# Hybrid mixer of a two-layer decoder: every second conv tile of the values and of the state space in another PSUM pool, with a new table of priority shifts

## The chip, the cores and the metric

The kernel runs on one core of one Trainium2 chip. The metric is the device time of one execution in microseconds, as the median of several runs. The profile is of one execution, taken by the hardware profiler.

## The reference

Two layers, 256 tokens of width 1024, in float32. Each layer is a feed-forward block, a mixer, and a second feed-forward block, each followed by a layer norm. Layer 0 has the hybrid mixer, which this case is about; layer 1 has a sparse attention.

```python
proj = x @ w_in                               # 256 x 1024 by 1024 x 5664
gdn_qkv, gdn_z, gdn_b, gdn_a, ssd_z, ssd_xbc, ssd_dt = split(proj)
# branch A: gated delta rule
qkv = silu(causal_conv(gdn_qkv, gdn_conv_w))  # 4 taps along the tokens, per channel
q, k, v = split(qkv)                          # 512, 512 and 1024 channels
o_a = rms_normalize(gated_delta_rule(q, k, v, g, beta)) * norm_w * silu(gdn_z)
# branch B: state-space scan
xbc = silu(causal_conv(ssd_xbc, ssd_conv_w) + ssd_conv_b)
xs, bm, cm = split(xbc)                       # 1024, 256 and 256 channels
o_b = rms_normalize((ssd_scan(xs, dt, a, bm, cm) + xs * d_skip) * silu(ssd_z)) * norm_w
return concat(o_a, o_b) @ w_out
```

## The kernel before

The whole computation is first written down as a list of operations (class Plan). Each operation belongs to an engine and has a priority, which is its place in the list plus a shift from the table SHIFTS: for each of the six stages (0 and 2 the feed-forward blocks of layer 0, 1 the hybrid mixer, 3 and 5 the feed-forward blocks of layer 1, 4 the attention) and each engine, a run-length list of (count, shift) over that engine's operations. A planner (Plan.order) then walks a cost model and, among the operations that are ready, gives each engine the one that can start first, and among equals the one with the lowest priority number. The result is a fixed order for each engine and a fixed place for each buffer; the chip then runs it with semaphores. So a change of a buffer's pool or of a shift moves the order of everything that follows.

PSUM's eight banks are three pools: ps with two banks, mp with two, acc with four. A tile takes a bank when its first operation is to start and gives it back after its last. Tiles of ps form one queue. Tiles of mp form one queue for each strand (STRANDS), all on the same two banks.

Matrices are split into a high and a low float32r part (whi, wlo from raw; x is held in the same way), and a product is three matmuls: high by high, high by low, low by high. Weights are loaded from DRAM by SP's queue into raw, rounded by ACT into whi, and VectorE makes wlo by subtraction.

In the hybrid mixer the keys and queries are projected and convolved first. Then five strands are woven together into the list (weave): delta (the delta rule's blocks, on acc), space, gate, space2 and out_a. Strand space holds the convolutions of this case: gdn_conv for the eight tiles of the values (128 channels each, 24 matmuls of 256 columns, tile by proj_steps), and then twelve state-space tiles (bm, cm and xs, by two_steps: eight matmuls of 512 columns and eight of 256). Each tile's bank is then read out by conv_tile: for a value tile ACT copies it to src; for a state-space tile ACT copies its second half and VectorE adds the first to it. The taps follow in SBUF (tiles cv). Strand gate makes the gate zs of the state-space branch, four tiles of 24 matmuls in ps, each read out by ACT. Strand space2 is the state-space scan; its products, and some of its transposes, are on mp. It waits until the xs tiles are there, and ends in the second half of the mixer's output, oT[1], which the last output matmuls of the mixer need.

turn is a transpose that does not use TensorE: ACT separates the float32 words into halves, a DMA from SP's queue transposes them, ACT puts them together.

Of the kernel before, what the change touches and what calls it, by code (L numbers as in the profile page):

```python
# [20 lines left out]
P = 128  # L21
# [31 lines left out]
        "tensor": [(18, -578), (1, 84), (2, -1851), (5, 0), (2, 407), (32, 0), (11, -1907), (2, 262), (32, 0), (22, 201), (5, 382), (5, 1394),  # L53
# [4 lines left out]
        "vector": [(2, -16), (1, 0), (4, 451), (1, 4), (1, -1802), (4, 0), (1, -739), (8, 0), (1, -2831), (3, 0), (8, 275), (1, 0), (2, 22), (7, 0),  # L58
            (1, -640), (1, 0), (1, -31), (12, -213), (2, 0), (18, -135), (1, -485), (1, -700), (4, 0), (12, -453), (6, 94), (3, 16), (1, -381),
            (2, -590), (5, 31), (3, 13), (4, 0), (6, -82), (1, -177), (3, -235), (2, 378), (4, -178), (10, -583)],  # L60
        "scalar": [(3, 756), (1, 0), (6, -699), (1, -20), (4, -2184), (2, 0), (2, -327), (6, -381), (1, -2057), (3, -1945), (1, -153), (12, 82),
            (2, 328), (1, -276), (1, -88), (1, -1), (2, -105), (2, -5), (4, 0), (1, -13), (2, -258), (16, 0), (1, -130), (2, 415), (1, 361),
            (1, -453), (12, 0), (2, 37), (14, 389), (1, -116), (1, 230), (2, 204), (4, -315), (1, -74), (7, -49), (1, -67), (2, -235), (5, -23),
            (2, 0), (10, -693)],
        "gpsimd": [(1, 451), (1, 0), (1, -714), (4, -48)],
        "sync": [(6, 0), (3, -1981), (1, -3772), (6, 0), (1, -85), (5, 1078), (2, 496), (1, 0), (56, 1116)],
    },
    1: {
        "tensor": [(218, 0), (26, -298), (75, 0), (2, 188), (1, 0), (1, 70), (1, 99), (2, 0), (4, -88), (4, 228), (1, 350), (2, -643), (29, 0),
# [10 lines left out]
        "vector": [(78, 0), (10, 241), (1, 3), (5, 408), (9, 40), (18, 0), (1, 273), (2, 293), (29, -903), (3, 392), (3, 504), (2, -456), (1, -320),  # L80
# [5 lines left out]
        "scalar": [(38, 0), (1, -321), (1, -310), (1, -130), (61, 0), (1, 520), (1, 322), (2, 0), (4, -46), (1, -21), (6, -66), (12, -449), (1, -10),  # L86
# [4 lines left out]
        "gpsimd": [(4, 57), (2, 43), (1, 53), (2, 0), (5, -40)],  # L91
        "sync": [(4, 297), (44, 0), (1, 452), (6, 230), (2, -3), (5, -355), (16, 3), (1, -364), (4, 0), (1, 6)],
    },
    2: {
        "tensor": [(74, 0), (1, -329), (1, -126), (2, -149), (9, 0), (1, -35), (5, 0), (1, -161), (5, 95), (20, -68), (2, 0), (9, 124), (8, -1221),
# [5 lines left out]
        "vector": [(30, 0), (1, -835), (1, 0), (1, -1084), (1, -565), (1, -599), (30, 0), (1, 98), (4, 72), (4, -1), (1, 35), (4, 768), (1, -608),  # L101
            (2, -480), (1, -541), (17, 42), (9, -118), (2, 0), (1, -101), (1, -146), (1, -144), (4, 0), (6, 871), (1, -135), (1, 1018), (7, 0),
            (2, 895), (7, 0), (1, -347), (2, -2074), (1, 0), (1, -1455), (5, -1745), (2, -1637), (1, -1605), (1, -2549), (1, 15), (1, -1586)],
        "scalar": [(10, 0), (22, 33), (3, -320), (1, 0), (35, 41), (1, -17), (2, -24), (1, -257), (13, 0), (1, 133), (5, 0), (3, -6), (1, -35),
            (5, -118), (5, -5), (5, -4), (1, 1040), (3, 42), (15, 0), (1, -175), (1, -348), (1, -1923), (1, -1471)],
    },
    3: {
        "tensor": [(3, 2), (22, 110), (7, 0), (2, 258), (1, -281), (18, 0), (2, 122), (23, 0), (2, -861), (8, 48), (1, -351), (139, -36), (1, 1919),
# [66 lines left out]
V_TURN, X_TURN = (1, 1), (1, 0)  # L175
O_TURN, Y_TURN, Q_TURN = (1, 1), (0, 1), (1, 1, 1, 1)
S_TURN = (0, 0, 1, 0, 0, 0, 1, 1)
L_TURN = (0, 0, 0, 0, 0, 0, 0, 0, 0, 0)
RUN = 1
MASKED = (1, 0)  # L180

# [610 lines left out]
class K:  # L792
# [1355 lines left out]
    def nsa(self, x, then):  # L2148
# [237 lines left out]
        def attend(g, b):  # L2386
# [3 lines left out]
            PT = {}  # L2390
# [235 lines left out]
```

## Time and profile before

| | |
|---|---|
| Median of 3 runs | 1056.72 us (1056.31 to 1056.89) |
| The profiled execution | 1058.01 us |
| Its span, first to last instruction | 1056.3 us |
| Instructions in the span | 15912 |
| Mean granted TensorE clock | 0.999 |

Engines in the profile: PE is TensorE's matmul, PEld its weight load (which overlaps PE), DVE is VectorE, ACT ScalarE, POOL GpSimd, SP SyncE. Operations are shown as out<-in by the names of the tiles. All operations are emitted by one helper, so they have one line (L757) and are told apart by their tiles. The row of a wait names who waited, for whom, how long in total, how often, and the longest. Times in rows are microseconds from the span's start unless ns is said. A float32 matmul or transpose is recorded as two matmuls, a float32r one as one.

### The profile page before, as it was taken

The page shows a single profiled execution, that of the slowest core. Times are in us where ns is not written, and L with a number is a line of the kernel's source. Part 1 is how long each engine was busy: PE and PEld are TensorE (multiplying, and loading weights), DVE is VectorE, ACT ScalarE, POOL GpSimd, SP SyncE. Part 2 cuts the span into 40 slices and gives each one's busy share as a digit, 9 for nine tenths or more (in the row PEclk, how much of TensorE's full clock was granted, in tenths as well). Part 3 has the DMA queues.
Part 4 walks back from the last instruction along what each step waited for, and adds up shares of the span by engine and source line. Part 5 has one row for each costly group of instructions (what it writes and reads, how often), then busy time and mean ns, then how long its engine had stood idle before and what let it go on. Part 6 is the DMA issues. An engine that isn't in the chain of part 4 may idle for free.

```text
span 1056.3 us, 15912 instructions
## 1 busy us (share of the span) xinstructions
PE 1043.7 (99%) x5686; PEld 868.4 (82%) x5686; DVE 1006.7 (95%) x1430; ACT 772.0 (73%) x1155; POOL 84.9 (8%) x122
## 2 busy tenths in 40 slices
PE   9999999999999999999999999999999999999997
PEld 7888888899898888888888888788887778888886
DVE  6999999898999989999999999999988999999987
ACT  7676976379867966868876678687477976878880
POOL 1001000001000201110000200000010101000100
PEclk9999999999999999999999999999999999999999
DMA  9999986744962798999779845978664355689991
GB/s 322 296 285 269 286 287 193 222 114 114 203 198 72 227 283 235 285 283 264 275 229 316 236 160 179 261 253 278 212 202 148 110 184 136 202 232 248 297 276 40
DMA packets 185977, 235.35 MB, mean 223 GB/s; under 512 B 54365, under 2 KB 115498, under 8 KB 185898
## 3 DMA queue, kind: packets, MB, share of 16 engines
q1 hardware_dynamic: 176650, 216.51, 65.1%
q0 software_dynamic: 9248, 17.83, 9.8%
q8 instruction: 45, 0.74, 0.3%
q14 instruction: 34, 0.28, 0.1%
HBM read 221.30 MB, written 1.07 MB: 211 GB/s over the span
## 4 chain that ended last, share of the span: by engine, by line
PE 52%; DVE 14%; ACT 3%; issue 3%; DMA 3%; POOL 1%; DVEq 0%; ACTq 0%; POOLq 0%
PE ps L757 18%; PE acc L757 18%; PE mp L757 15%; DVE wlo L757 5%; DMA turned<-words 2%; DVE cv L757 2%; ACT whi L757 2%; DVE arena L757 1%; DVE raw L757 1%; DVE h L757 1%; DMA G<-rates 1%; DVE qs L757 1%; DVE sw L757 0%; POOL arena L757 0%; DVE y L757 0%
## 5 line engine op out<-in xcount | busy, mean ns | idle before, releaser
L757 DVE TENSOR_TENSOR wlo<-raw,whi 128x1024 fp32r<-128x1024 f32 (+2 forms) x447 | 522.2, 1207 | 5.5 <-ACT whi L757 4.9
L757 ACT ACTIVATE whi<-raw 128x1024 fp32r<-128x1024 f32 (+1 forms) x428 | 424.0, 1044 | 53.0 <-DVE raw L757 37.3
L757 PE MATMUL ps<-whi,x 128*128 128x512 f32 (+1 forms) x544 | 144.2, 384 | 0.2 <-DVE F L757 0.2
L757 PEld LDWEIGHTS ps<-whi,x 128*128 128x128 f32 x544 | 98.2, 188 | 18.2 <-DVE x L757 0.3
L757 DVE TENSOR_TENSOR raw<-raw,raw 128x1024 f32<-128x1024 f32 x94 | 112.1, 1218 | 0.3
L757 PE MATMUL ps<-x,whi 128*128 128x512 f32 (+2 forms) x464 | 104.6, 340 | 0.7 <-ACT cv L757 0.3
L757 PE MATMUL acc<-wlo,gh 128*128 128x512 f32 x253 | 99.1, 392 | 0.2 <-DVE wlo L757 0.2
L757 PE MATMUL acc<-whi,gl 128*128 128x512 f32 x253 | 97.9, 392 | 0.0
L757 PE MATMUL acc<-whi,gh 128*128 128x512 f32 x253 | 95.9, 392 | 0.0
L757 PEld LDWEIGHTS ps<-x,whi 128*128 128x128 f32 (+1 forms) x464 | 77.6, 187 | 10.2 <-DVE cv L757 0.6
L757 PE MATMUL acc<-whi,x 128*128 128x512 f32 x256 | 82.1, 404 | 1.0 <-DVE x L757 1.0
L757 PE MATMUL mp<-whi,x 128*128 128x512 f32 x288 | 78.3, 391 | 0.0
L757 PE MATMUL ps<-wlo,x 128*128 128x512 f32 (+1 forms) x272 | 77.7, 380 | 0.0
L757 PE MATMUL mp<-whi,fhi 128*128 128x512 f32 x192 | 75.1, 391 | 0.3 <-ACT whi L757 0.3
L757 PE MATMUL mp<-whi,flo 128*128 128x512 f32 x192 | 74.8, 390 | 0.0
L757 POOL DMA_DIRECT2D raw<-in_ffn_w_in_dram x34 | 41.1, 1216 | 337.6 <-DMA raw<-in_ffn_w_in_dram 205.1
L757 PE MATMUL ps<-x,wlo 128*128 128x256 f32 (+1 forms) x344 | 66.5, 284 | 0.0
L757 PE MATMUL acc<-whi,g 128*128 128x512 f32 x192 | 63.4, 392 | 0.0
L757 PEld LDWEIGHTS mp<-whi,x 128*128 128x128 f32 x288 | 53.2, 188 | 11.7 <-ACT su L757 0.6
L757 PE MATMUL mp<-wlo,fhi 128*128 128x512 f32 x192 | 59.4, 392 | 0.1
L757 PEld LDWEIGHTS acc<-whi,x 128*128 128x128 f32 x256 | 47.8, 190 | 11.6 <-DVE x L757 1.4
L757 PEld LDWEIGHTS ps<-wlo,x 128*128 128x128 f32 x272 | 49.5, 188 | 8.7 <-DVE wlo L757 0.2
(330 smaller groups left out, 1850.3 us busy)
## 6 DMA issues: line engine op xcount, KB each, us to landing
raw<-in_ffn_w_in_dram SPq DMA_DIRECT2D x162, 512.0 KB, 6.2
raw<-in_ffn_w_out_dram SPq DMA_DIRECT2D x88, 512.0 KB, 6.1
raw<-in_hyb_w_in_dram SPq DMA_DIRECT2D x44, 512.0 KB, 5.4
raw<-in_ffn_w_in_dram POOLq DMA_DIRECT2D x34, 512.0 KB, 9.1
raw<-in_ffn_w_in_dram SPq DMA_DIRECT2D x52, 256.0 KB, 4.7
raw<-in_hyb_w_out_dram SPq DMA_DIRECT2D x16, 512.0 KB, 4.4
raw<-in_nsa_w_in_dram SPq DMA_DIRECT2D x10, 512.0 KB, 5.4
raw<-in_nsa_cmp_w_dram SPq DMA_DIRECT2D x8, 512.0 KB, 3.9
```

Source lines behind the costliest of these rows:

```text
L757: r = getattr(getattr(nc, eng), fn)(*[res(a) for a in args], **{k: res(a) for k, a in kw.items()})
```

## The change

Ten conv tiles move from ps to mp: of each pair of value tiles and of each pair of state-space tiles the second. Which pool each takes is now a table in the source, H_BANKS: two entries for the values, two for the state space, two for the z gate (both ps, as it was). The table of shifts is replaced as a whole, in all six stages and for all engines. Two further tables, R_TURN and P_TURN, would send the attention's rotated queries and its probabilities through turn in place of TensorE's transposes; all their entries are 0. For this turn takes a list of parts as well as one tile.

```diff
 SHIFTS = {
     0: {
-        "tensor": [(18, -578), (1, 84), (2, -1851), (5, 0), (2, 407), (32, 0), (11, -1907), (2, 262), (32, 0), (22, 201), (5, 382), (5, 1394),
+        "tensor": [(15, -61), (2, -377), (2, -329), (9, 0), (45, 343), (1, 0), (2, 8), (1, 17), (39, 0), (1, 686), (1, 0), (1, 9), (1, -376),
...
+R_TURN = (0, 0, 0, 0)
+P_TURN = (0, 0, 0, 0, 0, 0, 0, 0, 0, 0, 0, 0, 0, 0, 0, 0, 0, 0, 0, 0, 0, 0, 0, 0)
+H_BANKS = ('ps', 'mp', 'ps', 'mp', 'ps', 'ps')
...
     def turn(self, out, src):
-        n = src.ids.size // P
+        n = out.ids.size // P
...
-        self.nc.scalar.activation(w, src.words(), AF.Copy)
+        parts = src if isinstance(src, list) else [src]
+        k = n // len(parts)
+        for j, part in enumerate(parts):
+            self.nc.scalar.activation(w[:, :, j * k:(j + 1) * k], part.words(), AF.Copy)
...
     def z_gate_steps(self, x, w_in, c0, zs, gated):
...
             for b in range(2):
-                ps = self.bank("ps")
+                ps = self.bank(H_BANKS[4 + b])
...
         def space():
...
-            yield from gdn_conv("v", [(8 + n, vT[n // 4][:, n % 4, :]) for n in range(8)])
+            yield from gdn_conv("v", [(8 + n, vT[n // 4][:, n % 4, :]) for n in range(8)], H_BANKS[:2])
...
                 for e in range(2):
...
-                    ps = self.bank("ps")
+                    ps = self.bank(H_BANKS[2 + e])
                     yield from self.two_steps(x, w, ps)
```

The number of entries of the shift table, by stage, is 144, 279, 131, 71, 229 and 186 before, and 134, 289, 196, 146, 238 and 137 after. In stages 2 and 3 the table before had none for POOL and SP, the one after has.

More of the change, by code (lines that the diff above doesn't have):

```diff
@@ L61 @@
[L61 to L65, printed above, removed]
@@ L94 @@
-    2: {
-        "tensor": [(74, 0), (1, -329), (1, -126), (2, -149), (9, 0), (1, -35), (5, 0), (1, -161), (5, 95), (20, -68), (2, 0), (9, 124), (8, -1221),
[5 rows of a table removed]
[L101 to L105, printed above, removed]
-    },
@@ L107 @@
-    3: {
-        "tensor": [(3, 2), (22, 110), (7, 0), (2, 258), (1, -281), (18, 0), (2, 122), (23, 0), (2, -861), (8, 48), (1, -351), (139, -36), (1, 1919),
[3 rows of a table removed]
-        "vector": [(52, 0), (34, 1991), (2, 173), (4, 0), (6, 226), (4, 252), (4, -448), (2, 0), (1, -650), (3, -6), (2, -113), (3, 0), (36, 32)],
-        "scalar": [(58, 84), (1, -212), (21, 0), (18, 277), (1, -2210), (1, -2642)],
-    },
-    4: {
-        "tensor": [(1, 883), (6, 167), (6, 0), (13, 147), (88, 0), (2, 311), (2, 0), (1, -255), (1, 0), (1, -126), (6, 0), (2, -147), (1, 67),
[9 rows of a table removed]
-        "vector": [(1, -92), (24, 166), (1, 0), (1, 389), (2, 37), (1, 0), (10, 247), (1, -35), (1, -74), (1, 0), (2, -47), (28, 0), (1, 154),
-            (11, -1223), (11, 0), (2, 389), (1, 1045), (11, 292), (2, 323), (13, 0), (4, -238), (1, 39), (1, 0), (1, 649), (1, 0), (9, -41),
-            (1, -243), (15, 0), (2, 279), (13, 0), (5, -2869), (1, -88)],
-        "scalar": [(2, -359), (1, -15), (10, 29), (1, -268), (12, 0), (16, -37), (3, -79), (1, -270), (32, 0), (4, -372), (1, -48), (1, -169),
[3 rows of a table removed]
-        "gpsimd": [(10, 0), (3, -606), (1, 215), (2, 190), (16, 223), (27, -11), (12, -78)],
-        "sync": [(2, 42), (11, 202), (1, 0), (6, 16), (1, -31)],
-    },
@@ L136 @@
-    5: {
-        "tensor": [(44, 0), (2, -603), (1, 0), (2, -547), (1, -969), (3, -845), (4, -758), (5, 0), (1, -362), (2, -155), (6, 0), (1, -303), (17, 0),
[7 rows of a table removed]
-        "vector": [(1, 59), (1, -81), (8, 43), (2, 649), (2, 0), (2, 873), (1, 568), (3, -419), (1, -217), (1, -16), (2, 231), (1, 239), (3, 367),
-            (9, 0), (1, -13), (5, 314), (6, 41), (1, 3), (1, 2), (2, -1), (12, 194), (1, 6), (1, 412), (1, 203), (1, 0), (1, 239), (4, -735), (1, 0),
-            (5, -25), (1, 0), (5, -844), (8, -524), (9, 0), (2, -141), (1, 0), (3, 4837), (8, -233), (1, 72), (1, -8), (4, -26), (14, 12), (1, -435),
-            (3, -250), (7, -1440)],
-        "scalar": [(1, 59), (5, 44), (1, 1), (1, 13), (1, 30), (1, 0), (1, 256), (1, 245), (1, 0), (3, 1277), (1, 0), (4, 77), (3, 953), (1, 0),
-            (6, -110), (1, 231), (3, 362), (1, -167), (7, 0), (1, 315), (35, 0), (1, -864), (26, 0), (1, 124), (5, -449), (21, 0), (7, -1270),
-            (3, -1446), (2, -1431), (1, -427), (7, -479)],
-        "gpsimd": [(1, 315), (5, -62), (1, 2)],
-        "sync": [(20, 0), (1, -123), (20, 0), (3, -484)],
+        "tensor": [(15, -61), (2, -377), (2, -329), (9, 0), (45, 343), (1, 0), (2, 8), (1, 17), (39, 0), (1, 686), (1, 0), (1, 9), (1, -376),
[3 rows of a table added]
@@ new lines @@
+        "vector": [(7, 14), (2, -284), (4, 0), (1, -285), (47, 0), (2, -251), (1, 2), (1, -215), (10, 74), (2, 427), (1, 177), (1, 511), (1, 134),
+            (2, -138), (3, 892), (19, 11), (1, 0), (1, -182), (1, -210), (2, -197), (1, -124), (4, 0), (2, -371), (1, 192), (14, 0), (1, 351),
+            (5, 0), (5, -224), (4, -353), (1, -340), (1, 15), (1, -48), (1, -722), (11, -727), (1, -220)],
+        "scalar": [(11, 0), (1, -284), (2, 0), (1, -350), (1, -312), (1, 0), (2, -271), (3, -278), (1, -461), (25, 0), (1, -282), (1, -367),
+            (1, -922), (2, 0), (21, -262), (1, -119), (30, 1), (3, -338), (2, 0), (1, -94), (2, -168), (2, -149), (1, -138), (1, -146), (3, -180),
+            (2, -28), (7, 0), (2, -117), (2, 0), (10, -501), (1, -154), (1, -409), (1, -152), (2, 0), (1, -220)],
@@ new lines @@
+        "gpsimd": [(1, 75), (1, 246), (13, -159)],
+        "sync": [(6, 0), (7, -231), (1, -103), (2, -105), (1, -193), (5, 508), (1, 276), (1, 543), (1, 76), (56, 603)],
+    },
+    1: {
+        "tensor": [(1, 357), (250, 0), (2, 162), (2, 0), (1, -218), (63, 0), (2, 757), (29, 129), (1, 636), (3, 169), (13, -171), (1, -237), (1, 33),
[10 rows of a table added]
+        "vector": [(85, 0), (1, 231), (1, 0), (1, -189), (1, 2), (9, -105), (55, 0), (3, -806), (14, 73), (5, -993), (18, 0), (1, -441), (1, -398),
[4 rows of a table added]
+        "scalar": [(49, 89), (4, 0), (3, 78), (1, 138), (33, 0), (9, 140), (1, 122), (1, 125), (1, 154), (1, 144), (5, 0), (1, 114), (1, 125),
[4 rows of a table added]
+        "gpsimd": [(4, -105), (1, -108), (1, -13), (1, -299), (1, -320), (2, -41), (3, 20), (3, -4), (1, 68), (2, 3), (1, -1846), (1, -1029)],
+        "sync": [(7, 86), (53, 0), (17, -126), (1, -45), (1, -41), (4, 21), (14, -24)],
+    },
@@ new lines @@
+    2: {
+        "tensor": [(2, -96), (1, 74), (20, 0), (25, -836), (3, 0), (1, 179), (24, -294), (1, -121), (43, 0), (1, -339), (1, -555), (1, -596), (2, 0),
[7 rows of a table added]
+        "vector": [(1, -11), (1, -253), (2, 33), (1, -36), (1, 0), (1, -86), (1, 4), (6, -772), (1, -2), (1, -33), (1, -45), (2, -150), (15, 0),
[3 rows of a table added]
+        "scalar": [(5, -29), (1, 47), (3, -1144), (7, -331), (1, -285), (7, 0), (1, -144), (1, 0), (1, 414), (1, 0), (1, -6), (17, 0), (1, -117),
+            (2, -156), (11, -68), (1, -77), (1, 121), (3, 220), (9, 106), (9, 1620), (1, -68), (4, -27), (1, -22), (3, 1419), (1, 31), (7, -72),
+            (1, -636), (3, -597), (1, 3), (16, 0), (1, 503), (7, -42), (3, 286), (1, 174), (1, 6), (1, -119), (1, -91), (1, -304)],
+        "gpsimd": [(9, 0), (1, -17)],
+        "sync": [(39, 0), (46, 51)],
+    },
@@ new lines @@
+    3: {
+        "tensor": [(33, 0), (1, 80), (1, 208), (1, 0), (2, -26), (6, -161), (1, -516), (1, -520), (4, 399), (9, 0), (1, -529), (7, 0), (8, 581),
[6 rows of a table added]
+        "vector": [(2, -119), (1, -132), (3, 0), (1, 27), (1, 167), (3, 0), (1, 967), (14, 0), (1, 323), (1, -377), (1, 310), (4, 289), (1, -130),
+            (2, 1083), (2, 95), (5, 0), (37, -1729), (1, -164), (4, -91), (17, 304), (3, -128), (2, -76), (1, 0), (1, 70), (66, 0), (1, 152),
+            (1, 127), (3, 0), (2, 186), (1, 194), (2, 67), (1, 49), (1, 48)],
+        "scalar": [(1, 0), (1, -74), (1, -103), (27, 106), (2, 0), (1, 92), (3, 0), (2, 56), (1, 163), (2, 50), (1, 55), (2, 0), (1, -916),
+            (1, -128), (1, -67), (50, 0), (1, -404), (3, -194), (1, -564), (1, -142), (1, -546), (1, -384), (36, 0), (1, -295), (1, -21)],
+        "gpsimd": [(1, 84)],
+        "sync": [(20, 0), (3, 76), (1, 90), (60, -180)],
+    },
@@ new lines @@
+    4: {
+        "tensor": [(58, 881), (11, 0), (1, 98), (3, 0), (1, 445), (7, 271), (1, -22), (2, 57), (2, -20), (3, -200), (10, -6), (1, 0), (1, 19),
[7 rows of a table added]
+        "vector": [(1, 911), (1, 452), (1, 40), (3, 367), (2, 371), (1, 29), (1, 43), (1, 18), (1, 142), (3, 695), (1, 1018), (1, 0), (1, 374),
[4 rows of a table added]
+        "scalar": [(1, 547), (11, 0), (1, 279), (1, 345), (3, 0), (2, 40), (6, 840), (1, 0), (1, -178), (11, -259), (1, 0), (1, 174), (1, -114),
[3 rows of a table added]
+        "gpsimd": [(11, 0), (1, 1181), (2, 0), (1, 1348), (40, 0), (1, -57), (1, -4), (1, 239), (1, -48), (1, 193), (1, 272)],
+        "sync": [(12, 0), (1, 282), (20, 0), (1, 55), (7, 0), (2, -128), (1, 13), (1, 1)],
+    },
@@ new lines @@
+    5: {
+        "tensor": [(48, 1446), (5, 684), (2, 152), (21, 1868), (26, 0), (5, 212), (1, 65), (4, 552), (31, 0), (4, 215), (3, 195), (1, 156), (95, 0),
[4 rows of a table added]
+        "vector": [(11, 570), (1, 573), (1, 20), (1, 0), (1, 497), (1, 452), (1, -20), (4, -323), (1, 5), (2, -60), (1, -171), (39, 133), (6, 35),
[3 rows of a table added]
+        "scalar": [(6, 0), (1, 2), (1, 10), (1, 103), (1, 0), (1, 774), (6, 0), (1, 2), (1, -523), (7, -372), (4, -325), (63, 0), (1, -170),
+            (1, -202), (1, -367), (1, 338), (7, 0), (1, -136), (1, 100), (1, 142), (5, -231), (1, 22), (1, 28), (14, 0), (1, -497), (2, -487),
+            (1, -217), (1, -211)],
+        "sync": [(44, 0), (1, -525), (45, -31)],
@@ L2243, in queries @@
                 yield
-                pt = self.bank("mp")
-                for c in range(4):
-                    nc.tensor.transpose(pt[:, c * P:(c + 1) * P], q[b][:, g * 512 + c * P:g * 512 + (c + 1) * P], self.ident)
+                if R_TURN[2 * g + b]:
+                    pt = self.m4(512, "qr", "H")
+                    self.turn(H3(pt, 4), H3(q[b][:, gs], 4))
+                else:
+                    pt = self.bank("mp")
+                    for c in range(4):
+                        nc.tensor.transpose(pt[:, c * P:(c + 1) * P], q[b][:, g * 512 + c * P:g * 512 + (c + 1) * P], self.ident)
                 s = qs[b][g].rearrange("p (c two) t -> p c two t", two=2)
@@ L2440, in attend @@
                 for r in range(2):
-                    tq = None
                     for kb in range(b + 1):
                         yield
-                        pt = self.bank("mp")
-                        for n in range(4):
-                            nc.tensor.transpose(pt[:, n * P:(n + 1) * P], tiles[n // nh][:, n % nh, r, kb * P:(kb + 1) * P], self.ident)
-                        if b == 0:
-                            if r == 0:
-                                tl = self.m4(1024, "PT", "Q")
-                            dst = tl[:, r * 512:(r + 1) * 512]
-                        else:
-                            if kb == 0:
-                                tl = self.m4(1024, "PT", "Q")
-                            dst = tl[:, kb * 512:(kb + 1) * 512]
-                        self.copy(dst, pt)
+                        ks = slice(kb * P, (kb + 1) * P)
+                        if b == 0 and r == 0 or b and kb == 0:
+                            tl = self.m4(1024, "PT", "Q")
+                        o = (kb if b else r) * 512
+                        dst = tl[:, o:o + 512]
+                        if P_TURN[g * 12 + half * 2 + r + (4 + half * 2 + r + kb if b else 0)]:
+                            self.turn(H3(dst, 4), [t[:, :, r, ks] for t in tiles])
+                        else:
+                            pt = self.bank("mp")
+                            for n in range(4):
+                                nc.tensor.transpose(pt[:, n * P:(n + 1) * P], tiles[n // nh][:, n % nh, r, ks], self.ident)
+                            self.copy(dst, pt)
                         PT[half, r, kb] = dst
```

9 lines of the change are left out of this document (removed), and 108 rows, old and new, of the table SHIFTS.

## The prediction

> **What bounds the kernel now.** I read the page's first part, then the busy time by stretches, then the list of what TensorE waited for, then single rows around the banks that the change touches. Busy time of the three large engines:
>
> ```profile
> PE 1043.7 (99%) x5686; PEld 868.4 (82%) x5686; DVE 1006.7 (95%) x1430; ACT 772.0 (73%) x1155; POOL 84.9 (8%) x122
> ```
>
> TensorE works for 1043.7 of 1056.3 us. The stretches below are, in order, the opening, the first feed-forward block, the hybrid mixer (149 to 400), two feed-forward blocks, the core of the second mixer (775 to 875), and the last block with its end in a row of its own. Columns: busy time and count by engine, granted clock, DMA share, GB/s.
>
> ```profile
> 0.00:26.00 26.00, 24.10 (x95) 18.66 (x96) 17.95 (x26) 18.27 (x26) 4.47 (x25) 1.00 0.93 321
> 26.00:149.00 123.00, 123.00 (x564) 101.50 (x564) 121.16 (x128) 90.88 (x117) 9.77 (x8) 1.00 0.94 278
> 149.00:400.00 251.00, 249.38 (x1834) 219.25 (x1833) 236.39 (x455) 184.49 (x296) 17.89 (x27) 1.00 0.66 189
> 400.00:775.00 375.00, 374.57 (x1750) 309.27 (x1749) 368.19 (x442) 270.73 (x344) 26.92 (x27) 1.00 0.80 243
> 775.00:875.00 100.00, 98.96 (x659) 76.16 (x658) 93.73 (x190) 80.60 (x225) 11.37 (x22) 1.00 0.56 175
> 875.00:1000.00 125.00, 125.00 (x569) 103.35 (x568) 123.35 (x137) 100.00 (x123) 11.19 (x10) 1.00 0.81 222
> 1000.00:1056.30 56.30, 48.72 (x227) 40.23 (x225) 45.88 (x58) 27.08 (x31) 3.29 (x4) 0.98 0.57 162
> ```
>
> TensorE's idle time, stretch by stretch, is 1.90, 0, 1.62, 0.43, 1.04, 0 and 7.58 us, 12.57 in all. The 7.58 is the last layer norm and the output's transfer, behind the last matmul. What an order of instructions can win as idle time is 1.62 + 0.43 + 1.04 = 3.1 us, plus a part of the opening. In the hybrid mixer, where the banks change, it is 1.62 us of 251. The full list of TensorE's waits (us in total, times, longest):
>
> ```profile
> PE acc L757 <- POOL ones L757: 1.1, 1, 1.1
> PE acc L757 <- DVE x L757: 1.0, 2, 0.8
> PE mp L757 <- DVE arena L757: 0.5, 1, 0.5
> PE acc L757 <- DVE X L757: 0.5, 1, 0.5
> PE mp L757 <- ACT whi L757: 0.3, 1, 0.3
> PE ps L757 <- ACT cv L757: 0.3, 1, 0.3
> PE mp L757 <- DVE P L757: 0.3, 1, 0.3
> PE ps L757 <- DVE cv L757: 0.3, 1, 0.3
> PE ps L757 <- DVE F L757: 0.2, 1, 0.2
> PE acc L757 <- DVE wlo L757: 0.2, 1, 0.2
> PE ps L757 <- ACT zs L757: 0.2, 1, 0.2
> ```
>
> Three rows are waits for a ps bank to be read out by the conv or the z gate (cv twice, zs once): 0.3 + 0.3 + 0.2 = 0.8 us. That is all that TensorE visibly pays for having two ps banks there.
>
> **The change, part by part.** (1) Ten conv tiles, every second of the eight value tiles and of the twelve state-space tiles, go to an mp bank. Is one free? Busy time of the instructions on ps (first fence) and on mp (second) in the stretches of these convolutions; the columns are PE, PEld, DVE, ACT, clock, DMA.
>
> ```profile
> 243.00:304.00 61.00, 49.63 (x308) 43.60 (x306) 2.41 (x6) 5.95 (x15) 1.00 0.68 165
> ```
>
> ```profile
> 243.00:304.00 61.00, 0.00 (x0) 0.04 (x1) 0.00 (x0) 0.00 (x0) 1.00 0.68 165
> ...
> 337.00:362.00 25.00, 5.15 (x36) 4.71 (x36) 2.32 (x4) 0.00 (x0) 1.00 0.52 136
> ```
>
> Both mp banks stand empty from 243 to 304 while 49.63 us of matmuls go through ps; from 337 on the state-space scan uses mp itself. So the tiles find room, and the ps waits should go. What one such wait costs, from TensorE's own rows around two of them:
>
> ```profile
> 258.79 0.40 PE L757 MATMUL ps<-x,whi 128*128 128x256 f32 x2
> 259.02 0.28 PE L757 MATMUL ps<-x,wlo 128*128 128x256 f32 x1
> 259.48 0.39 PE L757 MATMUL ps<-x,whi 128*128 128x256 f32 x1 [0.18 <-ACT zs L757]
> ...
> 265.70 0.40 PE L757 MATMUL ps<-x,whi 128*128 128x256 f32 x2
> 265.94 0.28 PE L757 MATMUL ps<-x,wlo 128*128 128x256 f32 x1
> 266.53 0.50 PE L757 MATMUL ps<-x,whi 128*128 128x512 f32 x1 [0.31 <-ACT cv L757]
> ```
>
> Undisturbed, two 256-column matmuls start within 0.23 us, 0.12 each. Across the waits it is 0.46 and 0.59, so 0.34 and 0.47 are lost where the list shows 0.18 and 0.31: 0.16 more each, because the pipeline empties. The third wait, 0.26 by its row's finer figure (0.3 in the list), is taken in the same way at 0.42. Sum: 0.34 + 0.47 + 0.42 = 1.23 us gained. Bounds: nothing, if the new order has as many waits of another kind, and 1.23.
>
> (2) The evictions. These read a bank as before, with the same instructions:
>
> ```profile
> L757 ACT ACTIVATE cv<-ps x24: 358/374/388, 212.3 to 345.0; 128x256 f32<-128x256 f32 x24
> L757 DVE TENSOR_TENSOR cv<-ps,cv x12: 404/416/425, 273.8 to 345.7; 128x256 f32<-128x256 f32 x12
> ```
>
> Ten tiles' reads merely change from ps to mp; the four of the values are ACT's at 374 ns (median), the six of the state space have one on ACT and one on DVE. No count changes; cost 0. Matmuls, weight splits and DMAs are the same in number too.
>
> (3) The rest of the code. The two new tables of turns are all zero, so query and probability tiles still go through TensorE; the generalised turn helper gets one part and issues the same three instructions; the z gate's entry says ps as before. Cost 0, since nothing is issued.
>
> (4) The shifts are new in all six stages, for SP's and POOL's queues too, so the order changes everywhere. This is the part with no row. Its gain is bounded by the waits: without the opening's 1.1 and 0.8, ten waits of together 3.0 us remain in the list, by the rate above (0.16 each on top) 4.6 us with the pipeline's refills, of which 1.23 are counted already. So the redraw is worth at most about 3.4 us more, or 4.4 if the opening's 0.8 wait goes with its refill. On the side of loss, the feed-forward stretches hold no idle time to give (123.00 of 123.00, 125.00 of 125.00), but VectorE is at 121.16 and 123.35 there: a late split shows at once. The nearest price is a wait of the present list, 0.2 to 0.5, and ten of them, 4.6 us, equal to all that there are now. Between -3.4 and +4.6 I take 0, since the present order already has only ten short waits and nothing in the trace says that another will have fewer.
>
> The Trainium skill, on the page "TensorE: Matmul & The Clock Gate" (HAM oscillation — how this bites in real kernels), speaks against the change: cycling through PSUM banks can make TensorE idle briefly so often that its clock falls back. The rows above show a granted clock of 1.00 in every stretch up to 1000 us, the waits of 0.2 to 0.5 included, so the trace does not agree; were it to happen, one window of about 3.4 us (the page's figure) at half clock would cost 1.7 us, an estimate from that page.
>
> **The sum.** The profiled execution took 1058.01 us, its span 1056.3 plus 1.7 around it; the median of the runs is 1056.72, so 1.3 below. 1058.0 - 1.2 = 1056.8 for a profiled one, and 1056.72 - 1.2 = 1055.5 for the median. About 0.2% (2.1 us) is what a measurement of this kernel can tell from no change.
>
> **The rivals.**
> (a) *The ps waits were not worth anything*: TensorE takes the next ready instruction elsewhere, and ps has work but is no limit. For it: 1.62 us of idle time in 251. Time 1056.7.
> (b) *The redraw closes holes as well*: half of the other 3.4 us goes with the 1.2, 2.9 in all: 1053.8; with all of it and the opening's wait, 5.6 less: 1051.1. For it: the second mixer still idles 1.04 us and has two of the longest waits. Against: TensorE and VectorE cannot both be fuller in the feed-forward stretches.
> (c) *The scan waits for an mp bank* (slower). The scan ends the mixer. The chain that ended last, and a run of undisturbed matmuls for the rate:
>
> ```profile
> 372.12 5.92 DMA G<-rates
> ...
> 393.89 0.69 DVE x L757
> ...
> 394.63 5.51 PE acc L757 x23
> ...
> 448.17 8.19 PE mp L757 x36
> ```
>
> The next matmuls on the chain start at 394.63, right behind the scan's last piece of x: no slack is left, so the scan's delay becomes TensorE's idle time. A 512-column matmul takes 8.19/36 = 0.23 us, so one state-space conv tile fills its bank in 8 x 0.23 + 8 x 0.12 = 2.8 us at least. If the scan waits for one such fill, and the gain is used up by it, the time is 1056.7 + 2.8 = 1059.5. It decides from 2.1 us of delay (3.3 if the 1.2 is kept). Against it: ACT's last read of a conv bank (cv<-ps, above) is at 345.0, and mp had only 5.15 us of matmuls from 337 to 362.
> (d) *A load comes late in the opening* through SP's new shifts (slower). The first row has the DMA engines at 0.93 and 321 GB/s, so 0.52 MB out of turn is 1.6 us; two are 3.3 us, less the 1.2: 1058.8.
> (e) *TensorE has far more room than its busy time says.* In the mixer's row the weight loads are busy for 219.25 of 251 us, so 32 us would be free, and with a quarter of it won the time would be 1048.7. Against it: in the saturated stretch 26 to 149 the loads are busy for 101.50 of 123.00, 83%, and matmuls still follow each other without idle time; 83% is full here. The Trainium skill's "Perfetto Trace Analysis" (Identifying the Most-Contended Engine) has this rule, that weight-load time and not matmul time shows TensorE's headroom; the trace does not bear it out.
>
> **How the numbers follow.** Chances: the forecast 0.34, (a) 0.10, (b) 0.30, (c) 0.17, (d) 0.05, (e) 0.04. Within 0.2%: forecast and (a), 0.44. Faster: (b) and (e), 0.34. Slower: (c) and (d), 0.22. The likeliest case alone reaches from 1054.6 to 1057.2 (the bound of 2.1 us below, half a us of new waits above). The range takes in (b) with all its waits, 1051.0 (rounded), and (c) and (d) with half a microsecond beside it, 1060.0; (e) is left out, and with it the outer ends of (b) and (c).
>
> **What would show it.** Right: no more wait of TensorE for zs or cv behind a ps bank in the mixer, conv evictions cv<-mp ten in number, 1 to 1.5 us less idle time there, and the feed-forward stretches as full as before. (b) would show as idle time under 0.5 us between 775 and 875. (c) would show as waits of TensorE for x or y of the scan near 390, and of the scan's matmuls for cv. (d) would show as idle time above 1.9 us before 26, or as waits for raw. The prediction fails if the redraw moves the feed-forward stretches, where I have it at nothing.

## The result and the profile after

The changed kernel takes 1062.1 us (median of 5 runs, 1060.4 to 1065.21) against 1056.89 us of the kernel before (1056.31 to 1059.72): a ratio of 1.0051 with a 95% interval from 1.0039 to 1.0064. It is slower by 5.2 us, and 1055.5 was forecast. In a second session it took 1064.6 us (1063.24 to 1068.4), ratio 1.0081 [1.0060, 1.0101].

Its profiled execution took 1065.21 us, the span being 1063.1; that is 3.1 us above the median, so this trace shows somewhat more than the median loses. The page's first part, and busy time by the same stretches as before (busy time and count of PE, PEld, DVE, ACT, POOL; granted clock; DMA share; GB/s):

```profile
PE 1044.8 (98%) x5686; PEld 864.2 (81%) x5686; DVE 1006.8 (95%) x1416; ACT 776.7 (73%) x1160; POOL 92.0 (9%) x135
...
0.00:26.00 26.00, 23.10 (x98) 17.81 (x99) 18.82 (x26) 17.89 (x25) 4.51 (x25) 1.00 0.91 307
26.00:149.00 123.00, 122.87 (x561) 101.09 (x560) 120.30 (x128) 91.09 (x116) 9.81 (x8) 1.00 0.96 284
149.00:400.00 251.00, 246.86 (x1816) 214.74 (x1815) 233.71 (x450) 186.77 (x299) 18.13 (x27) 1.00 0.65 183
400.00:775.00 375.00, 373.44 (x1725) 306.54 (x1725) 367.97 (x432) 269.80 (x339) 28.41 (x29) 1.00 0.82 244
775.00:875.00 100.00, 98.14 (x668) 75.83 (x666) 89.57 (x181) 80.93 (x227) 14.51 (x32) 1.00 0.54 164
```

TensorE's idle time in the mixer is 4.14 us, where it was 1.62; in the feed-forward blocks behind it 1.56, where it was 0.43; in the second mixer 1.86, where it was 1.04; in the opening 2.90, where it was 1.90 (the last section comes back to that). The granted clock of the rows is the same. Most of the loss is idle time, and the largest piece of it is in the very stretch where 1.2 us were to be won. For some operations the planner also chooses the engine: VectorE has 14 instructions fewer than before and POOL 13 more, ten of them in the second mixer. TensorE's waits (us in total, times, longest):

```profile
PE acc L767 <- DVE x L767: 1.8, 2, 1.3
PE acc L767 <- ACT x L767: 1.2, 1, 1.2
PE acc L767 <- POOL ones L767: 1.1, 1, 1.1
PE acc L767 <- ACT whi L767: 1.1, 1, 1.1
PE mp L767 <- DVE P L767: 0.9, 1, 0.9
PE mp L767 <- DMA h<-in_x_dram: 0.8, 1, 0.8
PE ps L767 <- ACT whi L767: 0.7, 1, 0.7
PE ps L767 <- DVE wlo L767: 0.5, 1, 0.5
```

The three waits for cv and zs behind a ps bank are gone from the list (TensorE's single rows still have 0.13 us behind a ps bank and 0.08 behind an mp bank), and the ten tiles are read from mp:

```profile
L767 ACT ACTIVATE cv<-mp x10: 361/374/386, 245.2 to 345.2; 128x256 f32<-128x256 f32 x10
L767 DVE TENSOR_TENSOR cv<-mp,cv x6: 409/417/425, 283.1 to 348.2; 128x256 f32<-128x256 f32 x6
```

So the change did what it says. What came instead are waits for x, the input of the mixer's output product, and for weights (whi, wlo). To place them I gave each matmul the distance to the next one that its shape usually has in the trace of before, and called the sum up to an instruction its work (1016.6 us in all). The table says how many microseconds later than in the trace of before each trace reaches the same work; a step down a column is time lost there.

```
work (us)   after  after again   place
   140      -0.2       1.1       end of the first feed-forward block
   160       0.5       1.6       layer norm ahead of the mixer
   320       0.7       1.8
   380       3.7       3.3       mixer's end
   440       3.8       3.4
   500       6.6       5.6       first half of the feed-forward block behind it
   740       5.7       3.4
   940       7.1       4.7       second mixer and the block behind it
   end       6.7       4.6
```

Both executions lose in the same two places: 3.0 and 1.5 us at the mixer's end, of which about 2.2 in both by 360 us of work, and 2.8 and 2.2 us in the block behind it. From 500 to 740 some of it comes back, 0.9 and 2.2 us; the second mixer and the block behind it cost 1.4 and 1.3.

**The mixer's end.** Two single rows of TensorE in the trace after:

```profile
354.78 0.50 PE L767 MATMUL acc<-whi,x 128*128 128x512 f32 x1 [1.31 <-DVE x L767]
...
397.60 0.50 PE L767 MATMUL acc<-whi,x 128*128 128x512 f32 x1 [1.21 <-ACT x L767]
```

The first output products wait 1.31 us for x, which the delta rule's result becomes after its turn; the last wait 1.21 us for the state-space half, in this execution only. How the first comes about can be followed in the delta rule's last products and in the DMA transposes of its result, first before, then after (the numbers ahead of the comma are ns, the two behind it are the first and last start):

```profile
L757 PE MATMUL acc<-vn,DT x32: 273/275/275, 328.3 to 335.3; 128*128 128x128 f32 x32
...
341.87 4.02 SPq L757 DMA_TRANSPOSE turned<-words  x3
```

```profile
L767 PE MATMUL acc<-vn,DT x32: 270/275/275, 326.9 to 341.3; 128*128 128x128 f32 x32
...
347.45 5.03 SPq L767 DMA_TRANSPOSE turned<-words  x3
```

The 16 products (32 records) spread over 7 us before and over 14 after: in the new order conv and gate matmuls stand between them. The last starts 6.0 us later, the transposes 5.6.

**The block behind the mixer.** After: one load, a step of VectorE, two of TensorE, and SP's burst of nine loads (those issued between 435 and 462 us); behind it the same burst before:

```profile
456.90 12.73 DMA raw<-in_ffn_w_in_dram
...
469.73 1.22 DVE L767 TENSOR_TENSOR raw<-raw,raw 128x1024 f32<-128x1024 f32 x1 [1.87 <-DMA raw<-in_ffn_w_in_dram]
...
472.18 0.50 PE L767 MATMUL ps<-whi,fhi 128*128 128x512 f32 x1 [0.73 <-ACT whi L767]
...
473.88 0.74 PE L767 MATMUL ps<-wlo,fhi 128*128 128x512 f32 x2 [0.51 <-DVE wlo L767]
...
445.92 14.82 SPq L767 DMA_DIRECT2D raw<-in_ffn_w_in_dram  x9
```

```profile
439.64 17.62 SPq L757 DMA_DIRECT2D raw<-in_ffn_w_in_dram  x9
```

The burst begins 6.3 us later, 2.5 more than the mixer's own delay; a load out of it takes 12.73 us to land, VectorE waits 1.87 us for it, and TensorE then waits for splits of weights. By the distances of the table these two waits, 0.73 and 0.51, cost 0.89 and 0.67 us, 1.6 of the 2.8. In the second execution they are 0.31 and 0.50.

### The profile page after: what moved, and what is told of

Read it like the earlier page. It is cut to its first block, busy times and chain, and to the rows that moved or that the text cites. A ratio compares the mean times of both kernels' runs of the same rounds, so it can differ in the third digit from the quotient of the medians.

```text
span 1063.1 us, 15955 instructions
## 1 busy us (share of the span) xinstructions
PE 1044.8 (98%) x5686; PEld 864.2 (81%) x5686; DVE 1006.8 (95%) x1416; ACT 776.7 (73%) x1160; POOL 92.0 (9%) x135
## 4 chain that ended last, share of the span: by engine, by line
PE 63%; DVE 14%; issue 9%; DMA 9%; ACT 4%; POOL 1%; SPq 1%; DVEq 0%; POOLq 0%; ACTq 0%
PE acc L767 23%; PE mp L767 20%; PE ps L767 20%; DMA raw<-in_ffn_w_in_dram 6%; DVE wlo L767 5%; DMA turned<-words 2%; DVE raw L767 2%; ACT whi L767 1%; DVE cv L767 1%; DVE arena L767 1%; ACT P L767 1%; DMA raw<-in_hyb_w_out_dram 1%; SPq L767 1%; DVE X L767 1%; ACT sw L767 1%
## 5 line engine op out<-in xcount | busy, mean ns | idle before, releaser
L767 ACT ACTIVATE whi<-raw 128x1024 fp32r<-128x1024 f32 (+2 forms) x427 | 422.3, 1043 | 56.9 <-DVE raw L767 32.7
L767 PE MATMUL ps<-x,whi 128*128 128x512 f32 (+2 forms) x352 | 79.9, 340 | 0.2
L767 PEld LDWEIGHTS ps<-x,whi 128*128 128x128 f32 (+1 forms) x352 | 59.4, 186 | 7.9 <-ACT cv L767 0.3
L767 PEld LDWEIGHTS acc<-wlo,gh 128*128 128x128 f32 x253 | 47.5, 188 | 10.1 <-DVE wlo L767 0.2
```

Source lines behind the costliest of these rows:

```text
L767: r = getattr(getattr(nc, eng), fn)(*[res(a) for a in args], **{k: res(a) for k, a in kw.items()})
```

## The experiments

**Banks and shifts apart.** The question is which part of the change carries the time, the ten tiles on mp or the table. The four corners, each with one part of the change or none:

```diff
 banks_only:  SHIFTS of before;  H_BANKS = ('ps', 'mp', 'ps', 'mp', 'ps', 'ps')
 shifts_only: SHIFTS of after;   H_BANKS = ('ps',) * 6
 bare_ps:     SHIFTS = {};       H_BANKS = ('ps',) * 6
 bare_mp:     SHIFTS = {};       H_BANKS = ('ps', 'mp', 'ps', 'mp', 'ps', 'ps')
```

> The new banks with the old table of shifts in all six stages. Theory 'banks' (the ten conv tiles on mp are themselves what costs, 3.2 us at the hybrid mixer's end): about 1060, with the loss at that place alone. Theory 'table' (a table fits one course of the planner alone, and the new one is merely the worse draw): the old table meets another course from the mixer on, so clearly slower than the changed kernel, 1070 to 1100, the loss spread over the mixer and the stages behind it.

> The new table of shifts with all conv tiles on ps as before. Theory 'banks': the mixer's loss is gone, 1056 to 1059. Theory 'table': a table without its course, 1070 to 1100.

> No shifts at all, all conv tiles on ps: what the planner makes without a table, to be compared with the same on the new banks (next study). Theory 'table' (the table carries the time): 1090 to 1130. Theory 'banks': no more than some 10 us above the kernel before, since the table would then matter less than the place of the tiles.

> No shifts at all, the ten conv tiles on mp; to be read against the same on ps (bare_ps). Theory 'banks': slower than bare_ps by 3 us or more. Theory 'table': no steady sign, anything within 10 us either way of bare_ps, as each change of a bank draws another order.

Measured: banks_only 1089.02 us, ratio 1.0294 [1.0264, 1.0325]; shifts_only 1093.73, 1.0335 [1.0305, 1.0364]; bare_ps 1112.02, 1.0520 [1.0487, 1.0554]; bare_mp 1112.76, 1.0542 [1.0518, 1.0565]. Without any shifts the banks make no difference that can be told: 0.7 us between medians, with intervals of some 3 us either way that overlap. The table of before is worth 55 us (1112.02 to 1056.98), and a table fits one course only: put on the other banks, the two tables take 32 and 37 us more than the kernel before. A single row of TensorE in banks_only, and one of shifts_only, at the mixer's end:

```profile
375.29 0.76 PE L760 MATMUL acc<-whi,x 128*128 128x512 f32 x1 [12.87 <-DVE x L760]
```

```profile
365.26 0.50 PE L767 MATMUL ps<-whi,x 128*128 128x512 f32 x1 [2.41 <-DVE cv L767]
```

Not all of this is waiting. The mixer's rows of banks_only and shifts_only, and 5 us of banks_only inside its long wait:

```profile
149.00:400.00 251.00, 232.16 (x1720) 204.28 (x1719) 220.34 (x430) 171.55 (x271) 14.72 (x25) 0.95 0.58 161
...
370.00:375.00 5.00, 0.00 (x0) 0.00 (x0) 1.25 (x3) 5.00 (x7) 0.56 (x1) 0.50 0.58 111
```

```profile
149.00:400.00 251.00, 242.09 (x1722) 211.09 (x1721) 218.64 (x424) 164.98 (x260) 11.13 (x8) 0.95 0.59 172
```

The granted clock, 1.00 in the mixer before, is 0.95 in both, and 0.50 in the long wait. TensorE is busy for 1053.1 and 1061.1 us with the same 5686 matmuls, where it was 1043.7, and for 1067.0 in bare_ps: of the 32, 37 and 55 us, about 9, 17 and 23 are longer busy time, which goes with the lower clock, and the rest is idle time. So an order can pay for long waits twice. Which wait brings the clock down is not worked out here: in shifts_only it is at 0.50 from 315 to 325 us with no wait above 0.9 us in the 40 us before.

A shift is a number added to a place in a list. When the pool of ten tiles changes, the same numbers give another order, and TensorE waits 12.87 us for the delta rule's x. In shifts_only TensorE also waits 7.3 us in all for ps banks to be read out (cv 4.2 and 2.4, zs 0.7): that two ps banks cost next to nothing holds for the order of before, not for every order. So these two say nothing about the banks themselves; for that the order must stay.

**Only the mixer's shifts new.** New banks with the new table in the mixer alone, to see whether the loss is made by the shifts of the other five stages.

```diff
 SHIFTS of before, but SHIFTS[1] of after;  H_BANKS = ('ps', 'mp', 'ps', 'mp', 'ps', 'ps')
```

> New banks and the new shifts of stage 1 (the hybrid mixer), the old shifts in the other five stages. Theory 'banks': 1060, the mixer's 3.2 us more and nothing else. Theory 'table': the mixer starts from another course of stage 0 and hands another course to stage 2, so 1062 to 1085, with losses behind the mixer too.

Measured: 1069.77 us, 1.0116 [1.0092, 1.0140], slower than the whole change and within the range of 'table'. In the manner of the table above it loses 4.8 us between 380 and 400 and 7.5 from 440 to 740: the old shifts of the later stages do not fit a mixer that ends in another order.

**The same order, other banks.** A function behind the planner puts the ten tiles on mp and deals the two banks of each pool anew; each engine's order stays that of before.

```diff
+                    ps.t.moves = kind == "v" and e == 1     # and e == 1 for the state space
...
     order = plan.order({k: n for k, (n, _) in caps.items()})
+    rebank(order, MOVED)
```

> Every engine's instructions in exactly the order of the kernel before; only the place of the ten conv tiles is changed to mp afterwards (and ps and mp banks dealt out again to whichever comes free first). Theory 'table' (the banks are worth what the prediction's first step said, the order is what costs): the three waits behind a ps bank are gone and nothing else changes, 1.2 us faster, 1055 to 1056. Theory 'banks' (tiles on mp hinder the scan): 1059 to 1061, with waits at the mixer's end.

Measured: 1057.17 us against 1056.67, ratio 1.0002 [0.9993, 1.0010]. The banks are worth nothing that can be measured, though 1.23 us were booked for them; the interval, from 0.7 us faster to 1.1 slower, leaves no room for that. Neither theory's range (1055 to 1056, 1059 to 1061) was met. A run with the banks dealt anew and no tile moved was not made. The mixer's row, and two single rows of TensorE:

```profile
149.00:400.00 251.00, 248.71 (x1832) 218.63 (x1831) 235.91 (x455) 184.22 (x296) 17.91 (x27) 1.00 0.66 187
```

```profile
269.57 1.22 PE L757 MATMUL ps<-x,wlo 128*128 128x256 f32 x8 [0.68 <-DVE wlo L757]
...
291.09 2.06 PE L757 MATMUL acc<-X,AT 64*64 64x32 f32 x64 [0.69 <-DVE X L757]
```

The three ps waits are gone, and TensorE runs ahead only to wait a little later for VectorE: 0.68 us for a split, which is new, and 0.69 for the delta rule's X, where it was 0.47. The idle time of the stretch is 2.29 us, before 1.62. Both waits are there again, with the same lengths, in the trace of splice_mix further down, which has this order of the mixer on mp.

**Less work for VectorE.** Are the ps waits a lack of banks, or banks read out late by full engines? In the second case they go when VectorE has less to do; both theories expected them to stay or shrink. Both kernels leave out the 84 conv taps on VectorE, in the order of before.

```diff
+    order = [o for o in order if not (o[1] == "scalar_tensor_tensor" and o[2][0].t.name == "cv")]
     plan.emit(tc, pools, order)
```

> The kernel before in its own order, but VectorE's 84 tap instructions of the convolutions (28 tiles, three taps of 0.48 us each, 40 us in the mixer) are left out, so the convolutions have one tap. Control for the next run: what the ten tiles on mp are worth when VectorE has time to spare. 1055 to 1057 if TensorE sets the mixer's pace; by both theories the three waits behind a ps bank stay or shrink.

> The same without the taps, with the ten tiles on mp. Theory 'VectorE takes it back' (with the taps, what the free banks gave TensorE was lost again to VectorE's splits of the weights and to the delta rule's X, a row of 0.7 us each): without the taps 0.8 to 1.3 us faster than no_taps_ps in the mixer. Theory 'the banks were never worth it' (TensorE's stalls behind a ps bank are made good by the matmuls behind them anyway): within 0.4 us of no_taps_ps.

Measured: on ps 1055.79 us, 0.9966 [0.9950, 0.9983]; on mp 1054.49, 0.9961 [0.9947, 0.9976], against 1058.14 of before. The mixer's rows, ps then mp:

```profile
149.00:400.00 251.00, 249.77 (x1839) 220.29 (x1838) 208.35 (x372) 184.77 (x297) 17.67 (x27) 1.00 0.67 190
```

```profile
149.00:400.00 251.00, 250.07 (x1842) 220.38 (x1841) 208.86 (x375) 185.52 (x298) 17.67 (x27) 1.00 0.67 191
```

With 28 us less on VectorE (40 were expected) the idle time is 1.23 on ps and 0.93 on mp, and behind a ps bank 0.09 us of waiting is left on ps. In this order two ps banks are enough once the banks are read in time. What mp adds without the taps is not decided: the medians are 1.3 us apart, the ratios 0.5, with intervals that overlap, so neither theory of the second run is borne out or excluded. The Trainium skill, "Perfetto Trace Analysis" (Optimization Strategy), says that a gap which keeps coming back on the engine that should be saturated can mean too little PSUM for the next tile; here the gaps were behind PSUM banks, yet in this order neither these runs nor the same order on mp bear the rule out.

**Pulling the delta rule forward.** If the mixer's end is late because the last products vn by DT are, a lower priority number for these in the changed kernel should bring it back. Beside it the changed kernel itself ran once more.

```diff
-            (stage 1, tensor: the last four products acc<-vn,DT)  shift s
+            (stage 1, tensor: the last four products acc<-vn,DT)  shift s - 300
```

> The changed kernel with the last four products of the delta rule (the ones that ended 6 us later than before, and whose output the matmuls wait for at the mixer's end) 300 places earlier in priority, nothing else. Theory 'those four are late by themselves' : the wait of 1.3 us at 353 goes, 1060 to 1061. Theory 'table' (any one edit draws another course): 5 to 25 us slower than the changed kernel, in places that have nothing to do with the four.

> The changed kernel once more, for a second profile: are its losses (3.1 us at the mixer's end, 2.8 us in the next feed-forward block behind a late load) in every execution? By both theories the mixer's loss is, since it follows from the order; the load's may not be, and would then explain the wider spread of the runs. 1060 to 1064.

Measured: 1075.67 us, 1.0181 [1.0167, 1.0195], where the changed kernel beside it took 1064.6, just above the 1060 to 1064 expected of it. Rows of four_earlier:

```profile
L698 PE MATMUL acc<-vn,DT x32: 270/275/275, 325.9 to 337.8; 128*128 128x128 f32 x32
...
348.15 3.99 SPq L698 DMA_TRANSPOSE turned<-words  x3
...
356.64 0.76 PE L698 MATMUL acc<-whi,x 128*128 128x512 f32 x1 [3.99 <-DVE x L698]
```

The last products did come earlier, at 337.8 in place of 341.3, yet the transposes begin at 348.15 in place of 347.45, and the wait grew from 1.31 to 3.99 us. So the place of the last products does not set the wait by itself; the steps of VectorE and ACT between them and the transposes are part of it. Four numbers changed, and the planner put everything behind them in another order: a shift can't test a place. Orders themselves have to be put together.

**Two orders spliced.** splice() plans both tables in the source, takes each operation's start from one plan or the other by its stage, lays the two time scales together at the end of the mixer, and sorts. Banks as in the changed kernel.

```diff
+BEFORE_IN = (0, 1)                # splice_mix; (2, 3, 4, 5) in splice_rest
...
+    mine = [int(n not in BEFORE_IN) for n in stage]
+    spans = [plans[m].ops[n].start - end[m] for n, m in enumerate(mine)]
...
+    todo = sorted(plan.ops, key=lambda o: spans[o.idx])
```

> Order of the kernel before for the first feed-forward block and the mixer, order of the changed kernel for the four stages behind, on the changed kernel's banks (ten conv tiles on mp). Theory 'two places': the changed order loses 2.3 to 3.1 us at the mixer's end and 2.3 to 2.8 us in the feed-forward block behind it, each by its own order. Then only the second loss is left: 1056.7 + 2.5 + 0.5 = 1059.7 (1058.9 to 1060.5), and the mixer's stretch of the trace is as before. Theory 'one place': the block behind loses because the mixer's end hands it its buffers and loads late; then both losses go and it takes 1056.7 to 1057.7. Theory 'spread': the order has no place where the loss is made; then this is no faster than the changed kernel, 1062 or more.

> The counterpart: order of the changed kernel for the first feed-forward block and the mixer, order of the kernel before for the four stages behind. 'Two places': only the loss of the layer norm ahead of the mixer (0.6) and that of the mixer's end (2.3 to 3.1) are left: 1056.7 + 0.6 + 2.7 = 1060.0 (1059.4 to 1060.6). 'One place': both losses stay, 1062 to 1063. 'Spread': between before and after in no relation to the other splice, or slower than after.

Measured: splice_mix 1060.46 us, 1.0030 [1.0019, 1.0042]; splice_rest 1060.97, 1.0038 [1.0024, 1.0051]; before 1057.27. The times are those of "two places", each within or close to its range. The traces say something else about the second place. Rows of splice_mix (before's order up to the mixer's end): the delta rule's last products, TensorE behind the mixer, SP's burst:

```profile
L874 PE MATMUL acc<-vn,DT x32: 272/275/297, 329.4 to 336.5; 128*128 128x128 f32 x32
...
406.38 0.63 PE L874 MATMUL mp<-ident,h 128*128 128x128 f32 x4 [0.93 <-DVE h L874]
...
409.61 0.50 PE L874 MATMUL ps<-whi,x 128*128 128x512 f32 x1 [1.23 <-ACT x L874]
...
439.61 19.08 SPq L874 DMA_DIRECT2D raw<-in_ffn_w_in_dram  x9
```

Rows of splice_rest (the changed order up to the mixer's end):

```profile
L874 PE MATMUL acc<-vn,DT x32: 270/275/275, 326.5 to 340.9; 128*128 128x128 f32 x32
...
354.39 0.50 PE L874 MATMUL acc<-whi,x 128*128 128x512 f32 x1 [1.32 <-DVE x L874]
...
413.78 1.90 PE L874 MATMUL ps<-whi,x 128*128 128x512 f32 x7 [1.40 <-DVE x L874]
```

That the first place is made by the changed order of the mixer, and not by the banks, is shown: the wait of 1.31 us is there with that order (1.32) and not with that of before. In the manner of the table above, splice_rest loses 1.5 us from 320 to 360 of work, splice_mix nothing. The second place, 440 to 500, loses 0.1 in splice_mix and 0.0 in splice_rest: with the mixer of before the same feed-forward order issues its burst from 439.61, as before did (439.64), and not from 445.92. Between 430 and 520 VectorE waits 0.3 and 0.2 us in all for loads of this block's weights, where it waits 3.0 and 2.5 in the two executions of the changed kernel. So in the splices neither the new order of that block nor the changed mixer makes this loss by itself; that it needs both is likely, but not shown, since both splices instead lose 2.7 and 2.8 us between 380 and 420, at their seam, in the layer norm behind the mixer (0.93 and 1.23; 1.40), which neither whole kernel does: an end of one order and a start of another cover each other's latencies badly, and a stall there can give the loads behind it time. That their times met the numbers of "two places" is an accident of this seam.

**The table drawn on.** Some 6000 small trial moves in the shifts of each kernel, judged by the planner's own cost model. The tables that came of it differ from those they began with in all six stages.

```diff
 SHIFTS = {
-    (the changed kernel's, or that of before)
+    (the same, drawn on)
```

> The changed kernel with its table of shifts drawn on for some 6000 small trial moves by the planner's own cost model, the ten tiles on mp. Theory 'the draw': the banks are worth nothing and the 5 us are only a poorer draw of the table; then a further draw gives back most of it: 1058 to 1060. Rival 'the tiles on mp cost time that no order avoids': it stays at 1062 or more. If mp gave the planner room that ps has not, it falls under 1056.

> The same number of trial moves for the kernel before, with all tiles on ps: the version that may beat both. 'The draw': from a table that fits already a further draw gives little, 1055.5 to 1057 (within 0.2% of before). If the planner's model and the chip agree to better than 0.1%, it gains 0.7 us; if every new course costs some us on the chip, whatever the model says, it is at 1059 or more.

Measured: redraw_mp 1067.61 us, 1.0095 [1.0082, 1.0108]; redraw_ps 1059.88, 1.0024 [1.0013, 1.0035]. Both theories of a gain fall. On ps the redraw costs 2.6 us. On mp it brings nothing back: 1.0095, where the changed kernel had 1.0051 and 1.0081. Its time is in the range of the rival that the tiles on mp cost what no order avoids, but not for that reason: at the order of before the tiles cost nothing, and the largest loss is in a block without conv tiles. The last feed-forward block, in before, redraw_mp and redraw_ps, and two waits of redraw_mp there:

```profile
995.00:1030.00 35.00, 34.79 (x154) 28.45 (x153) 31.86 (x32) 30.21 (x34) 2.40 (x2) 1.00 0.98 286
```

```profile
995.00:1030.00 35.00, 31.34 (x131) 23.68 (x130) 29.70 (x28) 24.65 (x27) 2.40 (x2) 1.00 0.87 271
...
1011.95 0.50 PE L699 MATMUL ps<-whi,fhi 128*128 128x512 f32 x1 [1.54 <-ACT whi L699]
...
1015.31 0.51 PE L699 MATMUL ps<-whi,fhi 128*128 128x512 f32 x1 [1.36 <-ACT whi L699]
```

```profile
995.00:1030.00 35.00, 34.12 (x148) 27.32 (x147) 31.66 (x31) 28.96 (x32) 2.40 (x2) 1.00 0.93 288
```

Here the idle time is 0.21, 3.66 and 0.88 us: late weight splits in a feed-forward block once more, this time in the last one. In the mixer redraw_ps did close holes: its trace idles 0.77 us there, where it was 1.62. In the work table redraw_ps is 0.3 us ahead of before until 940 and loses 2.0 us from there to 980; redraw_mp keeps 2.8 until 940 and loses 5.0 there. No kernel tried here that computes the whole is faster than before.

## Why the prediction was wrong

- **Part (4), the shifts: the step that failed.** It took a redraw at 0 between -3.4 and +4.6 because no row showed that another order would have fewer or more waits. The runs show that zero was not the middle: the table carries 55 us, every other table tried on the whole computation cost between 2.6 us (redraw_ps) and 37 (shifts_only, a table put on other banks), and the change itself 5.2 and 7.9. An order with ten short waits in 1056 us is the best of those tried, and every other was worse. The end of +4.6 was too small as well: it came from counting waits of 0.2 to 0.5, while the new ones are 1.31, 1.21 and 0.73 + 0.51.
- **The feed-forward stretches, taken at nothing.** The prediction named this as the point on which it would fail, and it did: 2.8 and 2.2 us in the block behind the mixer. What it called a late split that shows at once was seen as 1.87 us of VectorE behind a load, then 0.73 and 0.51 us of TensorE.
- **Part (1), the banks: the mechanism seen, the size wrong.** The three ps waits went but for 0.13 us and ten evictions are from mp, as forecast. At constant order this is worth nothing to within about 1 us (1.0002 [0.9993, 1.0010]) and not 1.23. The refill of 0.16 per wait is borne out (0.73 and 0.51 cost 0.89 and 0.67 in the block behind the mixer); what failed is that a wait taken away was booked as time won. VectorE is at 94% of the mixer and sets the pace close behind, so TensorE waits for wlo, and longer for X, instead. Rival (a), which got 0.10, is what the banks alone did, by the reason that the prediction gave as a bound: as many waits of another kind.
- **Parts (2) and (3)**: no run singles out the cost of the evictions or the unused tables. The eviction medians stay at 372 to 374 and 414 to 417 ns. That no count changes holds for matmuls and evictions; VectorE's 14 instructions fewer and POOL's 13 more were not foreseen.
- **Rival (c), slower at the mixer's end, 0.17.** Place and size were close (2.8 us priced, 3.0 and 1.5 measured), the mechanism was not: no matmul of the scan waited for a conv tile on mp. The wait is for x of the delta rule. The splices show that the mixer's new order makes it; that it does so by spreading the last products is read from their rows, and four_earlier shows that this is not all. The second wait, 1.21 us for the state-space half, is in one of the two executions only.
- **Rival (b)**, that a redraw closes holes, shows in the mixer of redraw_ps alone and in no run's time; **(d)** has a 0.8 us wait for h in the opening, but the opening as a whole is no later in the first trace (-0.2) and 1.1 in the second; its sign, idle time above 1.9 us before 26, is met with 2.90 and tells nothing, since the order of before on mp has 2.68. **(e)** was not seen: PEld fell from 868.4 to 864.2 us, and TensorE won nothing by it. The clock stayed at 1.00 in every stretch up to 1000 us of the changed kernel, so the rule on bank cycling of the Trainium skill, "TensorE: Matmul & The Clock Gate" (A second HAM failure mode: psum-queue depth-cycling), which the prediction weighed, does not explain the loss. Where the clock did fall in the mixer, to 0.95 in banks_only and shifts_only, it is part of their loss.

What stays open: why the layer norm ahead of the mixer loses 0.5 to 0.7 us; which steps between the delta rule's products and its x make the wait; whether the loss behind the mixer needs the changed mixer as well as the new order; and the 1.3 to 1.4 us in and behind the second mixer, where the wait for P is 0.9 us in place of 0.3 and POOL has ten more instructions. Whether a table chosen by times on the chip could bring mp to or below ps wasn't tried.

## What to carry to other kernels

Time a change of resources at a fixed order first: here it takes one function behind the planner, and one run shows that the banks are worth nothing at that order. A wait is time to be won only if the engine behind the next one has room; here, with TensorE at 99% and VectorE at 95%, the closed gaps opened again a few microseconds later. And price a new order of a tuned kernel as a loss until it is timed: here its places were the handover between two blocks and the loads of a stretch with no idle time, and 6000 trial moves by the planner's own model did not win it back.

## What the runs showed that was not expected

The opening differs by more than a microsecond between executions of one order. In the profiled execution of the same order on mp TensorE is busy for 23.32 of the first 26 us, in that of before for 24.10, and after 20 us of work the first is 1.2 us ahead of the second; the two executions of the changed kernel are 1.3 us apart at the same place. TensorE's rows show where: the same two matmuls, first in before, then in the same order on mp:

```profile
7.20 1.42 PE L757 MATMUL acc<-whi,x 128*128 128x512 f32 x2
```

```profile
7.07 0.81 PE L757 MATMUL acc<-whi,x 128*128 128x512 f32 x2
```

In before the matmuls up to about 9 us take nearly twice as long as later ones, in the other execution only those up to about 4. The changed kernel's first execution is of the fast kind (0.82 for such a pair), its second of the slow kind (1.41), so this 1.3 us between them is not the order's. The clock column of the opening reads 1.00 in all of them. No run looked for what decides it.

And a 512 KB load took 12.73 us from issue to landing in the block behind the mixer, where the median of its kind in the same trace is 5.8 us from SP's queue and 8.4 from POOL's. Landings of that length are not the change's alone: of the loads issued between 440 and 485 us the longest took 12.0 us before and 14.3 after. Last, the granted clock falls to 0.50 in a wait of 12.87 us (banks_only), so that a badly ordered kernel loses more than its waits.
